# Convolution sums of an even mixer in PSUM, two taps per GpSimd add, and another order of its output projection

## The chip, the cores and the metric

The kernel runs on one core of a Trainium2 chip. The metric is the device time of one execution in microseconds (us); several runs are taken and their median is given. The engines are named as in the profile: PE is TensorE (matmuls; PEld its weight loads), DVE is VectorE, ACT is ScalarE, POOL is GpSimd, and SP issues most of the transfers.

## The reference

Two blocks on a sequence of 256 tokens of width 1024, in float32. The first block has two layers, each with a feed-forward part, a mixer and a second feed-forward part; the mixer of layer 0 is the even mixer, that of layer 1 a gated linear attention. The second block has one layer with two kinds of attention and a feed-forward part. The change touches the even mixer alone:

```python
def even_mixer(h, w_in, w_out, dw_w, dw_b, ln_g, ln_b):
    proj = h @ w_in
    q, k, v, u, gate = jnp.split(proj, [SB_WIDTH, 2 * SB_WIDTH, 3 * SB_WIDTH, 3 * SB_WIDTH + CONV_CH], axis=-1)
    a_out = merge_heads(stick_breaking_attention(
        split_heads(q, SB_HEADS), split_heads(k, SB_HEADS), split_heads(v, SB_HEADS)))
    c = u * jax.nn.sigmoid(gate)
    c = causal_depthwise_conv(c, dw_w, dw_b)          # 31 taps, 512 channels
    c = jax.nn.silu(layer_norm(c, ln_g, ln_b))
    return jnp.concatenate([a_out.astype(h.dtype), c], axis=-1) @ w_out
```

There are 8 heads of 64 columns. The attention and the convolution are independent of each other until the output projection, which takes the heads as the first 512 of its input rows and the convolution as the other 512.

## The kernel before

**Products.** Every float32 product of the large projections is made of three matmuls: each operand is split into a rounded part and the rest (hi and lo of a weight, xh and xl or mh and ml of an activation), and hi·high, lo·high and hi·low are summed in PSUM (lines 269, 270, 271).

**Weights.** They arrive in chunks of 512 KB. For a chunk SP issues the transfer into one of four buffers `raw` (line 226), ACT writes `hi` (line 246), DVE writes `lo` = raw − hi (line 247), and the buffer takes the transfer of the chunk four places on as soon as its `lo` is done. `nxt` hands chunks to the matmuls and, each time, converts ahead up to a distance that `DEPTH` gives; while `side` holds `conv_some`, each chunk that is handed over also issues some taps of the convolution.

**The order** in which each engine gets its instructions is the order of the program (`manual_schedule`); an engine waits at an instruction until its operands are there, with all that stands behind it.

**The even mixer** runs from about 204 to 325 us of the span. A projection by `wp` is 48 matmuls. First come the convolution's inputs (`hu`, `hg`, twice, for the channel groups 0, 1 and 2, 3 of 128 channels each); behind the first pair stands `rows`, which turns the row scales of the input's norm into a tile `rb` by two small matmuls (line 432) of diagonal tiles `dg` from ACT (line 431). The gated product goes into `cpad` (line 829). Then `qk(0)` and `qk(1)` project queries and keys (`qT` line 844, `kT` line 847), and the attention runs over four pairs of heads: `z_` (logits, on PE from qT and kT, line 856), `e_` (ACT: abs, exp, ln; DVE: max and add, line 873), `c_` (sums of logarithms on PE, exp on ACT), `o_` (the values on PE, `mh` by ACT line 897, `ml` by DVE line 898).

The 31 taps of each channel group are laid between these steps by the numbers in TD, TP, TC and TE. Groups 0 and 2 run on DVE alone: even taps sum into `y`, odd ones into `yb` (line 793, both in SBUF), and the last step adds the two (line 795). Groups 1 and 3 run on two engines: ACT multiplies one tap (line 803) and POOL adds it to `y` (line 804).

**The end of the mixer.** `part` issues the first piece of the output projection (chunk rows of `mh` 0 and 1, all four of its PSUM banks: 24 matmuls, in the order hi·mh, lo·mh, hi·ml for each). Then the last taps, `c_(2)`, `c_(3)`, `conv_mean` (PE sums over channels, line 905; DVE subtracts, line 907; ACT squares), `o_(2)`, `o_(3)`, `conv_var` (layer norm, silu on ACT, and the split into mh and ml, lines 532 and 533), a second `part`, and the rest in `pieces`. PSUM has 8 banks, handed out in turn by `pb()`.

Of the kernel before, what the change touches and what calls it, by code (L numbers as in the profile page):

```python
# [12 lines left out]
AF = mybir.ActivationFunctionType  # L13
ALU = mybir.AluOpType
AX = mybir.AxisListType.X

S = 256
# [5 lines left out]
CW = 31  # L23
# [4 lines left out]
NH = 3  # L28
TB = (5, 6)
KO = (0, 4, 1, 5, 2, 6, 3, 7)  # L30
TD, TP, TC = (3, 2), 3, ((5, 6), (5, 6), (4, 6), (4, 5))
PRE = (1, 1, 2)
PRT = ((0, 0, 0), (1, 0, 0))
PRF = (0, 0, 2)
CT, CS = (2, 2), (0, 1)
CU = (0, 1, 2)
DEPTH = (14, (10, 9), (10, 10), (10, 10))
NT = 2
LO, CL = ((1, 0), (1, 1)), 1
PG = 5  # L40
# [3 lines left out]
NW = 8  # L44
KS = (1, 3, 5, 7)
TE = (2, 0, 4, 4)
W2 = dict(qa=0, ka=512, va=1024, iq=1536, ik=2048, iw=2112, qr=2120, kr=2632,
          vr=3144, gr=4168, ga=5192, gb=6216)

# [51 lines left out]
def weight_plan(a):  # L101
    plan = []

    def cols(name, w, c0, n, k0=0, nk=8):
        plan.append((name, w[k0 * 128:(k0 + nk) * 128, c0:c0 + n].rearrange("(k p) c -> p k c", p=128), nk, n))

    def tall(name, w, c0):
        for k0 in (0, 4):
            cols(name, w, c0, 256, k0, 4)

    def wide(name, w, c0=0, n=1024, nk=8):
        for cc in range(c0, c0 + n, 512):
            for k0 in range(0, nk, 2):
                cols(name, w, cc, 512, k0, 2)
# [41 lines left out]
    w = a["w_in_2"]  # L156
    wide("va", w, W2["va"], 512)
    wide("rv", w, W2["vr"], 512)
    cols("ik", w, W2["ik"], 72)
    for c in range(2):  # L160
        tall("iq", w, W2["iq"] + 256 * c)
    for c in range(2):
        tall("rq", w, W2["qr"] + 256 * c)
        tall("rk", w, W2["kr"] + 256 * c)
    wide("rv", w, W2["vr"] + 512, 512)
# [23 lines left out]
def block_kernel(ctx: ExitStack, tc: tile.TileContext, a: dict, out: bass.AP, upto: int = 99):  # L189
    nc = tc.nc  # L190
    pe, act, dve, pool = nc.tensor, nc.scalar, nc.vector, nc.gpsimd
# [8 lines left out]
    def pb():  # L200
        return ps.tile([128, 512], F32, tag="pb", name="pb")

    def pp():
        return [pb(), pb()]
# [4 lines left out]
    def s4(shape, dt=F32, name="s4"):  # L209
        return wk.tile(shape, dt, tag="s4", name=name, bufs=NS4)  # L210

    def s2(shape, dt=F32, name="s2"):
        return wk.tile(shape, dt, tag="s2", name=name, bufs=NS2)
# [3 lines left out]
    raw_t, cv_t = {}, {}  # L217
    pos = {"dma": 0, "cv": 0, "use": 0, "depth": DEPTH[0]}
    side = []
# [31 lines left out]
    def nxt(*names, ahead=True):  # L251

        i = pos["use"]
        for d_, nm in enumerate(names):
            assert plan[i + d_][0] == nm, (plan[i + d_][0], nm)
        n = i + len(names)
        feed_cv(max(n, min(i - 1 + pos["depth"], pos["cv"] + len(names) + 1)) if ahead else n)
        pos["use"] += len(names)
        for _ in names:
            for f in list(side):  # L260
                f()
        r = [cv_t.pop(i + d_) for d_ in range(len(names))]
        return r if len(r) > 1 else r[0]
# [4 lines left out]
    def mm3(o, lh, ll, rh, rl, start, stop):  # L268
        pe.matmul(o, lh, rh, start=start, stop=False)  # L269
        pe.matmul(o, lh, rl, start=False, stop=False)  # L270
        pe.matmul(o, ll, rh, start=False, stop=stop)  # L271

    def tsl(t):
        return slice(t * 128, (t + 1) * 128)
# [276 lines left out]
    def two(z):  # L551
        return z.rearrange("p (c s) -> p c s", c=2)
# [4 lines left out]
    def smm(o, t, ch, k0, nk, xh, xl):  # L557
        for k in range(ch[0].shape[1]):
            kk = k0 + k
            mm3(o, xh[:, kk, tsl(t)], xl[:, kk, tsl(t)], ch[0][:, k], ch[1][:, k], kk == 0, kk == nk - 1)  # L560
# [21 lines left out]

    def sproj_tail(name, xh, xl):

        f = [pp(), pp()]
        pos["depth"] = DEPTH[0]
        todo = {t: {n: [0, 1, 2, 3] for n in range(2)} for t in range(2)}
        chs = {}

        def one(t, n, i):  # L590
            smm(f[t][n], t, chs[i][n], 2 * i, 8, xh, xl)

        def part(leave=()):

            i = len(chs)
            chs[i] = nxt(name, name)
            for t in range(2):
                for n in range(2):
                    if (t, n) not in leave:
                        todo[t][n].remove(i)  # L600
                        one(t, n, i)

        def pieces():
            i0 = len(chs)
            cs = nxt(*[name] * (2 * (4 - i0)), ahead=False)
            for i in range(i0, 4):
                chs[i] = cs[2 * (i - i0):2 * (i - i0) + 2]
            return lambda t: [(lambda n=n, i=i: one(t, n, i)) for n in range(2) for i in todo[t][n]]
        return f, part, pieces
# [3 lines left out]
    part = const.tile([128, 192], F32, name="part")  # L613
# [143 lines left out]
    def even_mixer(nz):  # L757
# [17 lines left out]
        for c in range(4):  # L775
            pool.memset(cpad[c][:, :CW - 1], 0.0)
        y = s4([128, 4, S], name="y")
        yb2 = s2([128, 2, S], name="yb")
        yb = [yb2[:, c] for c in range(2)]
        dq, aq, pts = [], [], []  # L780

        def tap(c, k, on_dve):
            src = cpad[c][:, k:k + S]
            w = cols_[:, 1, 4 * k + c:4 * k + c + 1]
            b = cols_[:, 2, 24 + c:25 + c]
            if on_dve:
                o = yb[c // 2] if k % 2 else y[:, c]
                if k == 0:
                    dve.tensor_scalar(o, src, w, b, op0=ALU.mult, op1=ALU.add)
                elif k == 1:  # L790
                    dve.tensor_scalar(o, src, w, None, op0=ALU.mult)
                else:
                    dve.scalar_tensor_tensor(o, in0=src, scalar=w, in1=o, op0=ALU.mult, op1=ALU.add)
                if k == CW - 1:
                    dve.tensor_tensor(o, o, yb[c // 2], op=ALU.add)
            elif k == 0:
                act.activation(y[:, c], src, AF.Identity, scale=w, bias=b)
            else:
                if not pts:
                    p2 = s2([128, 2, S], name="pt")  # L800
                    pts.extend([p2[:, 0], p2[:, 1]])
                pt = pts.pop(0)
                act.activation(pt, src, AF.Copy, scale=w)
                pool.tensor_tensor(y[:, c], y[:, c], pt, op=ALU.add)

        calls = []

        def conv_some(n=None, m=TP):
            if n is None:
                n = TD[len(calls) % len(TD)]  # L810
                calls.append(n)
            for q, n_ in ((dq, n), (aq, m)):
                for _ in range(min(n_, len(q))):
                    tap(*q.pop(0))

        for c in range(2):
# [15 lines left out]
            if c == 0:  # L832
                side.append(conv_some)
        pos["depth"] = DEPTH[1][1]
        act.preload_act_table_set("natural_log_exp_and_others")
# [28 lines left out]
        def e_(hp):  # L864
            pz = st[hp]
            e = s4([128, 2, 384], name="ze")
            for i in range(2):
                act.activation(e[:, i], pz[i][:, :384], AF.Abs)
            act.activation(e, e, AF.Exp, scale=-1.0)
            act.activation(e, e, AF.Ln, bias=1.0)  # L870
            conv_some(TE[hp], 0)
            for i in range(2):
                dve.scalar_tensor_tensor(e[:, i], in0=pz[i][:, :384], scalar=0.0, in1=e[:, i],
                                         op0=ALU.max, op1=ALU.add)
            st[hp] = pz, e
# [68 lines left out]
        z_(3)  # L944
        o_(1)
        f, part, pieces = sproj_tail("ho", mh, ml)
        e_(2)
        conv_some(*TC[3])
        e_(3)
        part()  # L950
        conv_some(99, 99)
        y2 = s4([128, 4, S], name="y2")
        c_(2)
        c_(3)
# [1 line left out]
        o_(2)  # L956
        o_(3)
        conv_var()
        part(LO)
        return f, pieces()  # L960


    def odd_mixer(nz):
        x = nz.x
        pos["depth"] = DEPTH[2][1]
        sc_ = s4([128, 2, 4, 128], name="scores")
# [197 lines left out]
        for t in range(2):  # L1164
# [3 lines left out]
            gated(t, 1)  # L1168
            rows_T(t, oy[t], oh, ol, [0])
        f, part, pieces = sproj_tail("go", oh, ol)  # L1170
        part()
        for t in range(2):
# [5 lines left out]
    def second(nz):  # L1178
# [315 lines left out]
        for t in range(2):  # L1494
            rows_T(t, ga[t], xh3, xl3)
        f, _, pieces = sproj_tail("wo", xh3, xl3)
        return f, pieces()

# [31 lines left out]
    for k in range(8):  # L1530
        nz.evac1(0, k)
        for i in (k // 4 * 2, k // 4 * 2 + 1):
            hi, lo = (z[:, k % 4] for z in cv_t[i])
# [7 lines left out]
    for i in range(6):  # L1541
        l, s = divmod(i, 3)
        gb = brow(a["norm_g"][l, 2 * s + 1])
        if s == 1:
            pos["depth"] = DEPTH[1 + l][0]
            f, pieces = (odd_mixer if l else even_mixer)(nz)
        else:
            f, pieces = ffn(nz, each)
# [11 lines left out]
        if upto == i:  # L1560
            dump()
            return
    pos["depth"] = DEPTH[3][0]
    f, pieces = second(nz)
# [9 lines left out]
    f, pieces = ffn(nz)  # L1574
    for t in range(2):
# [5 lines left out]
        y = [s2([128, 512], name="tm") for _ in range(2)]  # L1581
# [33 lines left out]
```

## Time and profile before

| | |
|---|---|
| median of 3 runs | 1476.81 us (1474.69 to 1477.07) |
| the profiled execution | 1476.34 us |
| its span, and its mean granted clock of PE | 1474.6 us, 0.992 |
| PE busy | 1440.0 us, 98% |
| PEld busy | 1314.8 us, 89% |
| DVE busy | 1000.3 us, 68% |
| ACT busy | 764.5 us, 52% |
| POOL busy | 259.5 us, 18% |

The span is the time between the first and the last instruction of the profiled execution; 1.7 us of its own time lie around it. Busy shares are means over all stages, and the even mixer is some 8% of the span.

### The profile page before, as it was taken

The page shows a single profiled execution, that of the slowest core. Times are in us where ns is not written, and L with a number is a line of the kernel's source. Part 1 is how long each engine was busy: PE and PEld are TensorE (multiplying, and loading weights), DVE is VectorE, ACT ScalarE, POOL GpSimd, SP SyncE. Part 2 cuts the span into 40 slices and gives each one's busy share as a digit, 9 for nine tenths or more (in the row PEclk, how much of TensorE's full clock was granted, in tenths as well). Part 3 has the DMA queues.
Part 4 walks back from the last instruction along what each step waited for, and adds up shares of the span by engine and source line. Part 5 has one row for each costly group of instructions (what it writes and reads, how often), then busy time and mean ns, then how long its engine had stood idle before and what let it go on. Part 6 is the DMA issues. An engine that isn't in the chain of part 4 may idle for free. (4 is left out here: it accounts for less than half of the span.)

```text
span 1474.6 us, 24444 instructions
## 1 busy us (share of the span) xinstructions
PE 1440.0 (98%) x9623; PEld 1314.8 (89%) x9623; DVE 1000.3 (68%) x1348; ACT 764.5 (52%) x1182; POOL 259.5 (18%) x339
## 2 busy tenths in 40 slices
PE   9999998699999999999999999999999999999997
PEld 8999988579999999999888899998988877899997
DVE  6777658977776667766577677765596865566542
ACT  6554356756543364443663655545643664565431
POOL 3010025812000031000234110001132230200001
PEclk9999999899999999999999999999999999999999
DMA  8887644227887568775542488763565554387540
GB/s 276 275 279 250 188 144 130 71 86 241 286 260 234 172 223 265 231 237 173 163 144 72 129 282 261 259 207 116 164 198 169 165 170 157 101 262 240 183 129 29
DMA packets 194948, 281.03 MB, mean 191 GB/s; under 512 B 12381, under 2 KB 148241, under 8 KB 194834
## 3 DMA queue, kind: packets, MB, share of 16 engines
q1 hardware_dynamic: 184386, 248.87, 53.5%
q0 software_dynamic: 10048, 30.03, 6.2%
q8 instruction: 75, 1.23, 0.3%
q10 hardware_dynamic: 400, 0.57, 0.1%
q14 instruction: 39, 0.32, 0.1%
HBM read 277.90 MB, written 1.05 MB: 189 GB/s over the span
## 5 line engine op out<-in xcount | busy, mean ns | idle before, releaser
L247 DVE TENSOR_TENSOR lo<-raw,hi 128x1024 fp32r<-128x1024 f32 (+1 forms) x461 | 549.5, 1219 | 237.2 <-ACT hi L246 204.0
L246 ACT ACTIVATE hi<-raw 128x1024 fp32r<-128x1024 f32 (+1 forms) x472 | 477.4, 1037 | 206.4 <-PE pb L271 69.2
L269 PE MATMUL pb<-xh,hi 128*128 128x256 f32 x1968 | 558.4, 284 | 0.1
L271 PE MATMUL pb<-xh,lo 128*128 128x256 f32 x1968 | 556.8, 283 | 0.0
L270 PE MATMUL pb<-xl,hi 128*128 128x256 f32 x1968 | 556.8, 283 | 0.0
L269 PEld LDWEIGHTS pb<-xh,hi 128*128 128x128 f32 x1968 | 376.3, 191 | 3.4 <-issue 1.3
L270 PEld LDWEIGHTS pb<-xl,hi 128*128 128x128 f32 x1968 | 376.4, 191 | 2.0
L271 PEld LDWEIGHTS pb<-xh,lo 128*128 128x128 f32 x1968 | 376.3, 191 | 0.2
L269 PE MATMUL pb<-hi,hh 128*128 128x512 f32 x440 | 172.1, 391 | 0.0
L270 PE MATMUL pb<-lo,hh 128*128 128x512 f32 x440 | 171.7, 390 | 0.0
L271 PE MATMUL pb<-hi,hl 128*128 128x512 f32 x440 | 171.2, 389 | 0.0
L626 POOL DMA_DIRECT2D ada<-in_w_ada_dram x96 | 51.8, 542 | 452.0 <-PE pb L271 278.8
L532 ACT ACTIVATE hh<-u 128x512 fp32r<-128x512 f32 x50 | 31.6, 632 | 134.4 <-DVE u L745 132.5
L271 PEld LDWEIGHTS pb<-hi,hl 128*128 128x128 f32 x440 | 82.6, 188 | 17.5
L269 PEld LDWEIGHTS pb<-hi,hh 128*128 128x128 f32 x440 | 82.8, 188 | 15.9
L270 PEld LDWEIGHTS pb<-lo,hh 128*128 128x128 f32 x440 | 82.8, 188 | 15.3
L269 PE MATMUL pb<-hi,xh 128*128 128x512 f32 x224 | 91.5, 408 | 0.0
L271 PE MATMUL pb<-hi,xl 128*128 128x512 f32 x224 | 88.1, 393 | 0.0
L270 PE MATMUL pb<-lo,xh 128*128 128x512 f32 x224 | 88.0, 393 | 0.0
L730 ACT ACTIVATE sg<-sg 128x512 f32<-128x512 f32 x40 | 25.3, 632 | 109.8 <-DVE sg L729 109.8
L631 DVE SCALAR_TENSOR_TENSOR adacc<-ada,sc,adacc 128x512 f32<-128x512 f32 x84 | 63.0, 750 | 2.0
L331 POOL TENSOR_TENSOR rs_y<-rs_v,mhalf 128x1 f32<-128x1 f32 x30 | 16.9, 564 | 259.0 <-DVE rs_v L330 258.0
(314 smaller groups left out, 1726.2 us busy)
## 6 DMA issues: line engine op xcount, KB each, us to landing
raw<-in_ffn_w_in_dram SPq DMA_DIRECT2D x176, 512.0 KB, 5.0
raw<-in_ffn_w_out_dram SPq DMA_DIRECT2D x88, 512.0 KB, 4.7
raw<-in_w_in_dram SPq DMA_DIRECT2D x56, 512.0 KB, 4.2
ada<-in_w_ada_dram POOLq DMA_DIRECT2D x96, 256.0 KB, 4.5
raw<-in_gla_w_in_dram SPq DMA_DIRECT2D x24, 512.0 KB, 4.2
raw<-in_w_ffn_gate_dram SPq DMA_DIRECT2D x22, 512.0 KB, 4.8
raw<-in_w_ffn_up_dram SPq DMA_DIRECT2D x22, 512.0 KB, 5.0
raw<-in_w_ffn_down_dram SPq DMA_DIRECT2D x22, 512.0 KB, 4.0
```

The lines of the kernel that those rows point to most:

```text
L246: act.activation(hv, r, AF.Copy)
L247: lo_on.tensor_tensor(lv, r, hv, op=ALU.subtract)
L269: pe.matmul(o, lh, rh, start=start, stop=False)
L270: pe.matmul(o, lh, rl, start=False, stop=False)
L271: pe.matmul(o, ll, rh, start=False, stop=stop)
L331: pool.tensor_tensor(y, v, mhalf[:, :1], op=ALU.pow)
L532: act.activation(hi, full, AF.Copy)
L626: pool.dma_start(t, w_ada[kt * 128:(kt + 1) * 128, cb * 512:(cb + 1) * 512])
L631: dve.scalar_tensor_tensor(ada["acc"], in0=t, scalar=sc[:, kt:kt + 1], in1=ada["acc"], op0=ALU.mult, op1=ALU.add)
L730: act.activation(sg, sg, AF.Silu)
```

## The change

Six things:

1. A DVE group's two sums stand in one PSUM bank (its two halves of 256 columns) instead of in SBUF. The last tap and the closing add write `y` in SBUF.
2. An ACT group's taps go in pairs: ACT writes two products side by side (`pt`, 512 columns), and one POOL add of 512 columns puts them on a pair of sums `ya`; two adds of 256 columns close the group.
3. The first `part` uses three of the four banks of the output projection and issues all its matmuls with `mh` ahead of those with `ml`: 12, and then 6. The second `part` leaves out the same bank (18 matmuls instead of 12), and the banks are taken from the pool one by one as they are first used.
4. The last taps are issued ahead of that `part`, so ahead of the conversions in it.
5. TC lays the taps between the steps a little differently.
6. `DEPTH` of the first two projections rises from 10 to 12.

```diff
-TD, TP, TC = (3, 2), 3, ((5, 6), (5, 6), (4, 6), (4, 5))
+TD, TP, TC = (3, 2), 3, ((5, 6), (4, 6), (3, 6), (4, 6))
...
-DEPTH = (14, (10, 9), (10, 10), (10, 10))
+DEPTH = (14, (12, 9), (10, 10), (10, 10))
...
+HL = ((1, 1),)
...
-        f = [pp(), pp()]
+        f = [[None, None], [None, None]]
...
+        def bank(t, n):
+            f[t][n] = f[t][n] or pb()
+            return f[t][n]
+
         def one(t, n, i):
-            smm(f[t][n], t, chs[i][n], 2 * i, 8, xh, xl)
-
-        def part(leave=()):
+            smm(bank(t, n), t, chs[i][n], 2 * i, 8, xh, xl)
+
+        def part(leave=(), low_last=False):
 
             i = len(chs)
             chs[i] = nxt(name, name)
...
+            tn = [(t, n) for t in range(2) for n in range(2) if (t, n) not in leave]
+            for t, n in tn:
+                todo[t][n].remove(i)
+                if not low_last:
+                    one(t, n, i)
+            for low in range(2 if low_last else 0):
+                for t, n in tn:
+                    o = bank(t, n)
+                    for k in range(2):
+                        kk = 2 * i + k
+                        hi, lo = (z[:, k] for z in chs[i][n])
+                        if low:
+                            pe.matmul(o, xl[:, kk, tsl(t)], hi, start=False, stop=kk == 7)
+                        else:
+                            pe.matmul(o, xh[:, kk, tsl(t)], hi, start=kk == 0, stop=False)
+                            pe.matmul(o, xh[:, kk, tsl(t)], lo, start=False, stop=False)
...
         def tap(c, k, on_dve):
...
             if on_dve:
-                o = yb[c // 2] if k % 2 else y[:, c]
+                if k == 0:
+                    acc[c] = two(pb())
+                o = acc[c][:, k % 2]
...
+                elif k < CW - 1:
+                    dve.scalar_tensor_tensor(o, in0=src, scalar=w, in1=o, op0=ALU.mult, op1=ALU.add)
                 else:
-                    dve.scalar_tensor_tensor(o, in0=src, scalar=w, in1=o, op0=ALU.mult, op1=ALU.add)
-                if k == CW - 1:
-                    dve.tensor_tensor(o, o, yb[c // 2], op=ALU.add)
+                    dve.scalar_tensor_tensor(y[:, c], in0=src, scalar=w, in1=o, op0=ALU.mult, op1=ALU.add)
+                    dve.tensor_tensor(y[:, c], y[:, c], acc.pop(c)[:, 1 - k % 2], op=ALU.add)
             elif k == 0:
-                act.activation(y[:, c], src, AF.Identity, scale=w, bias=b)
+                acc[c] = [s2([128, 2, S], name="ya"), None]
+                act.activation(acc[c][0][:, 0], src, AF.Identity, scale=w, bias=b)
+            elif k == 1:
+                act.activation(acc[c][0][:, 1], src, AF.Copy, scale=w)
+            elif k < CW - 1:
+                ya = acc[c][0]
+                if k % 2 == 0:
+                    acc[c][1] = s2([128, 2, S], name="pt")
+                pt = acc[c][1]
+                act.activation(pt[:, k % 2], src, AF.Copy, scale=w)
+                if k % 2:
+                    pool.tensor_tensor(ya, ya, pt, op=ALU.add)
             else:
...
-                pool.tensor_tensor(y[:, c], y[:, c], pt, op=ALU.add)
+                pool.tensor_tensor(pt, ya[:, 1], pt, op=ALU.add)
+                pool.tensor_tensor(y[:, c], ya[:, 0], pt, op=ALU.add)
...
-        part()
         conv_some(99, 99)
+        part(HL, True)
...
-        part(LO)
+        part(HL)
```

Three places show how the order of instructions moves. On ACT, ahead of the diagonal tiles of `rows` (the second projection of the mixer is being multiplied on PE then), before:

```order
L773 ACTIVATE cr<-zmf 128x384
L246 ACTIVATE hi<-raw 128x1024 x3
L431 ACTIVATE dg<-ident,rs_y 128x128 x2
L827 ACT_TABLE_LOAD
L827 ACTIVATE sgg<-sgg 128x512
L246 ACTIVATE hi<-raw 128x1024 x2
```

and in the changed kernel, whose line numbers are one to some thirty higher:

```order
L789 ACTIVATE cr<-zmf 128x384
L247 ACTIVATE hi<-raw 128x1024 x5
L432 ACTIVATE dg<-ident,rs_y 128x128 x2
L853 ACT_TABLE_LOAD
L853 ACTIVATE sgg<-sgg 128x512
L247 ACTIVATE hi<-raw 128x1024 x2
```

Two more conversions stand ahead of `dg`. On DVE, up to the first `kT`, before:

```order
L793 SCALAR_TENSOR_TENSOR y<-cpad,cols,y 128x256
L844 SCALAR_TENSOR_TENSOR qT<-pb,rb 128x512
L247 TENSOR_TENSOR lo<-raw,hi 128x1024 x2
L793 SCALAR_TENSOR_TENSOR yb<-cpad,cols,yb 128x256
L793 SCALAR_TENSOR_TENSOR y<-cpad,cols,y 128x256
L793 SCALAR_TENSOR_TENSOR yb<-cpad,cols,yb 128x256
L793 SCALAR_TENSOR_TENSOR y<-cpad,cols,y 128x256
L793 SCALAR_TENSOR_TENSOR yb<-cpad,cols,yb 128x256
L847 TENSOR_TENSOR kT<-pb,rb 128x512
L247 TENSOR_TENSOR lo<-raw,hi 128x1024 x2
```

and in the changed kernel:

```order
L809 SCALAR_TENSOR_TENSOR pb<-cpad,cols,pb 128x256 x5
L870 SCALAR_TENSOR_TENSOR qT<-pb,rb 128x512
L248 TENSOR_TENSOR lo<-raw,hi 128x1024
L809 SCALAR_TENSOR_TENSOR pb<-cpad,cols,pb 128x256 x5
L873 TENSOR_TENSOR kT<-pb,rb 128x512
L248 TENSOR_TENSOR lo<-raw,hi 128x1024 x2
```

The number of taps between is the same and one conversion is gone from between (`pb` is the PSUM bank). On DVE at the end of the mixer, before:

```order
L873 SCALAR_TENSOR_TENSOR ze<-pb,ze 128x384 x2
L247 TENSOR_TENSOR lo<-raw,hi 128x1024 x3
L793 SCALAR_TENSOR_TENSOR yb<-cpad,cols,yb 128x256
L793 SCALAR_TENSOR_TENSOR y<-cpad,cols,y 128x256
L793 SCALAR_TENSOR_TENSOR yb<-cpad,cols,yb 128x256
L793 SCALAR_TENSOR_TENSOR y<-cpad,cols,y 128x256
L795 TENSOR_TENSOR y<-y,yb 128x256
L907 TENSOR_TENSOR y<-y,pb 128x256 x4
```

and in the changed kernel:

```order
L899 SCALAR_TENSOR_TENSOR ze<-pb,ze 128x384 x2
L809 SCALAR_TENSOR_TENSOR pb<-cpad,cols,pb 128x256 x5
L811 SCALAR_TENSOR_TENSOR y<-cpad,cols,pb 128x256
L812 TENSOR_TENSOR y<-y,pb 128x256
L248 TENSOR_TENSOR lo<-raw,hi 128x1024 x3
L933 TENSOR_TENSOR y<-y,pb 128x256 x4
```

The three conversions now stand behind the last tap and ahead of the subtraction of the mean, instead of ahead of the last four taps.

## Rows read from the trace of the kernel before

**Rows 1.** Waits of PE over the whole span: total us, times, longest

```profile
PE pb L856 <- DVE kT L847: 9.0, 2, 7.3
PE pb L271 <- DVE ml L898: 6.4, 2, 3.8
PE pb L1081 <- DVE last L1057: 2.1, 1, 2.1
PE pb L269 <- ACT mh L532: 1.2, 1, 1.2
```

**Rows 2.** Windows: PE, PEld, DVE, ACT, POOL busy (x); PEclk, DMA share, GB/s

```profile
254.00:306.60 52.60, 36.43 (x218) 28.75 (x218) 52.57 (x70) 36.02 (x71) 38.29 (x43) 0.87 0.24 73
...
261.20:265.20 4.00, 3.96 (x18) 2.86 (x18) 4.00 (x4) 2.21 (x4) 3.80 (x3) 0.50 0.35 115
...
291.70:295.70 4.00, 4.00 (x10) 3.13 (x11) 4.00 (x7) 3.93 (x6) 3.61 (x6) 0.50 0.00 0
```

**Rows 3.** Timelines of DVE and PE up to the second kT: start, length

```profile
236.75 2.89 DVE L247 TENSOR_TENSOR lo<-raw,hi 128x1024 fp32r<-128x1024 f32 x2
...
247.22 1.23 DVE L247 TENSOR_TENSOR lo<-raw,hi 128x1024 fp32r<-128x1024 f32 x1 [1.61 <-ACT hi L246]
...
256.18 0.94 DVE L793 SCALAR_TENSOR_TENSOR yb<-cpad,cols,yb 128x256 f32<-128x256 f32 x1
...
260.51 0.68 DVE L847 TENSOR_TENSOR kT<-pb,rb 128x512 f32<-128x512 f32 x1
...
261.24 1.65 PE L856 MATMUL pb<-qT,kT 64*128 64x256 f32 x8 [7.29 <-DVE kT L847]
...
279.76 0.92 PE L856 MATMUL pb<-qT,kT 64*128 64x256 f32 x8 [1.74 <-DVE kT L847]
```

**Rows 4.** Timelines of POOL and DVE at the mixer's end

```profile
270.51 28.31 POOL L804 TENSOR_TENSOR y<-y,pt 128x256 f32<-128x256 f32 x31 [3.31 <-ACT pt L803]
...
287.73 0.41 DVE L898 TENSOR_TENSOR ml<-pb,mh 128x256 fp32r<-128x256 f32 x1
...
301.54 3.48 DVE L247 TENSOR_TENSOR lo<-raw,hi 128x1024 fp32r<-128x1024 f32 x3
...
305.74 0.47 DVE L793 SCALAR_TENSOR_TENSOR yb<-cpad,cols,yb 128x256 f32<-128x256 f32 x1
306.13 0.47 DVE L793 SCALAR_TENSOR_TENSOR y<-cpad,cols,y 128x256 f32<-128x256 f32 x1
306.64 0.42 DVE L795 TENSOR_TENSOR y<-y,yb 128x256 f32<-128x256 f32 x1
308.29 1.41 DVE L907 TENSOR_TENSOR y<-y,pb 128x256 f32<-128x256 f32 x4 [1.22 <-PE pb L905]
```

**Rows 5.** Groups of POOL's adds by shape: busy, mean ns of one

```profile
L804 POOL TENSOR_TENSOR y<-y,pt 128x256 f32<-128x256 f32 x60 | 54.7, 912 | 31.3 <-ACT pt L803 26.8
...
L1342 POOL TENSOR_TENSOR sgr<-sgr,brow 128x512 f32<-128x512 f32 x4 | 5.2, 1291 | 25.1 <-ACT sgr L1341 25.0
...
L1069 POOL TENSOR_TENSOR ex<-cs 128x512 f32<-128x512 f32 x6 | 10.5, 1751 | 0.0
```

**Rows 6.** Timelines of ACT, PE and DVE around the diagonal tiles

```profile
218.90 2.94 ACT L246 ACTIVATE hi<-raw 128x1024 fp32r<-128x1024 f32 x3
...
224.20 0.60 PE L432 MATMUL pb<-dg,ones 128*128 128x128 f32 x4
...
228.63 0.76 DVE L829 TENSOR_TENSOR cpad<-sgg,us 128x256 f32<-128x256 f32 x2 [2.04 <-ACT sgg L827]
```

**Rows 7.** Transfers of line 226 from 195 to 262: issues, time to landing

```profile
221.23 2.64 SPq L226 DMA_DIRECT2D raw<-in_hyb_w_in_dram  x3
...
DMA to landing us min/median/max: 3.5/4.6/5.6
```

**Rows 8.** Windows behind PE's wait at line 1081 (columns as in rows 2)

```profile
766.00:768.00 2.00, 1.85 (x10) 1.73 (x11) 2.00 (x4) 0.58 (x1) 0.00 (x0) 0.76 0.40 156
768.00:770.00 2.00, 2.00 (x6) 1.57 (x5) 2.00 (x4) 0.04 (x2) 0.00 (x0) 0.50 0.21 14
```

More of the change, by code (lines that the diff above doesn't have):

```diff
@@ L588, in sproj_tail @@
         chs = {}
+        def bank(t, n):
+            f[t][n] = f[t][n] or pb()
+            return f[t][n]
         def one(t, n, i):
-            smm(f[t][n], t, chs[i][n], 2 * i, 8, xh, xl)
-        def part(leave=()):
+            smm(bank(t, n), t, chs[i][n], 2 * i, 8, xh, xl)
+        def part(leave=(), low_last=False):
             i = len(chs)
             chs[i] = nxt(name, name)
[L597 to L601, printed above, removed]
+            tn = [(t, n) for t in range(2) for n in range(2) if (t, n) not in leave]
[14 more added lines that the diff above has]
+                            pe.matmul(o, xh[:, kk, tsl(t)], lo, start=False, stop=False)
         def pieces():
@@ L777, in even_mixer @@
         y = s4([128, 4, S], name="y")
-        yb2 = s2([128, 2, S], name="yb")
-        yb = [yb2[:, c] for c in range(2)]
-        dq, aq, pts = [], [], []
+        dq, aq, acc = [], [], {}
         def tap(c, k, on_dve):
@@ L791, in tap @@
                     dve.tensor_scalar(o, src, w, None, op0=ALU.mult)
-                else:
-                    dve.scalar_tensor_tensor(o, in0=src, scalar=w, in1=o, op0=ALU.mult, op1=ALU.add)
-                if k == CW - 1:
-                    dve.tensor_tensor(o, o, yb[c // 2], op=ALU.add)
+                elif k < CW - 1:
+                    dve.scalar_tensor_tensor(o, in0=src, scalar=w, in1=o, op0=ALU.mult, op1=ALU.add)
+                else:
+                    dve.scalar_tensor_tensor(y[:, c], in0=src, scalar=w, in1=o, op0=ALU.mult, op1=ALU.add)
+                    dve.tensor_tensor(y[:, c], y[:, c], acc.pop(c)[:, 1 - k % 2], op=ALU.add)
             elif k == 0:
-                act.activation(y[:, c], src, AF.Identity, scale=w, bias=b)
-            else:
[L799 to L802, printed above, removed]
+                acc[c] = [s2([128, 2, S], name="ya"), None]
[10 more added lines that the diff above has]
+                    pool.tensor_tensor(ya, ya, pt, op=ALU.add)
+            else:
+                ya, pt = acc.pop(c)[0], s2([128, S], name="pt")
                 act.activation(pt, src, AF.Copy, scale=w)
-                pool.tensor_tensor(y[:, c], y[:, c], pt, op=ALU.add)
+                pool.tensor_tensor(pt, ya[:, 1], pt, op=ALU.add)
+                pool.tensor_tensor(y[:, c], ya[:, 0], pt, op=ALU.add)
         calls = []
```

## The prediction

> **What bounds the kernel now.** The page comes first: PE is busy 98% of the span, so only PE's idle time and the time it runs at a low clock can be won. The list of PE's waits then says where they are [rows 1]: the four waits for `kT` and `ml` (15.4 us), and one of 1.2 us for `mh`, all lie in the even mixer. Who is late there is seen in the windows [rows 2]: from 254 to 306.6 us DVE is busy 52.57 of 52.60 us, PE 36.4, and the granted clock is 0.87. [...]
>
> Why DVE is late is read from its single instructions. A tap takes 0.94 us while POOL adds [rows 3] and 0.47 when POOL has stopped, with one starting every 0.39 [rows 4]. POOL adds nearly without a gap (31 in 28.31 us). A tap alternates between `y` and `yb`, so it never follows the tap whose sum it needs; where one does follow its own producer (the closing add behind the last tap) the start is 0.51 behind [rows 4]. A DVE instruction with one operand in PSUM takes the same beside POOL as an SBUF add without it: `ml` 0.41 at 287.73, against 0.42 for the closing add [rows 4].
>
> **The change, part by part.**
>
> *Taps in PSUM.* What is not in the trace is a DVE instruction that writes PSUM. Both halves of a bank belong to one tile, and in the built program each tap waits for the tap right ahead of it. I take 0.51 a tap, the start-to-start of the dependent pair, with no slowing by POOL, since only `cpad` is left in SBUF, and the row with one PSUM operand shows none. Lower bound 0.39 (dependence hidden); upper bound 0.88, today's start-to-start beside POOL (0.94 less the overlap of 0.06), should POOL still get in the way. The value lies near the low end because the `ml` row does.
>
> [...]
>
> *The rows step (DEPTH).* Ahead of `dg` ACT now converts five chunks instead of three. The three took 2.94 us [rows 6], 0.98 each. The fifth chunk waits for its transfer: the first of the three issues at 221.23 [rows 7], when a buffer is free. Landing takes 3.5 to 5.6 us there, median 4.6; I take 4.2, a little under it, because fewer transfers are under way at that place than later in the stretch. Landed 225.4, converted 226.4, `dg` +0.44: PE's matmul of line 432, which ran at 224.20 without a wait [rows 6], now starts at 226.85. **PE waits 2.65 us** (2.0 to 4.1 over the range of landings). Behind it in PE's queue stand the second `hu` and all of the rest; `rb`, and with it all DVE work of the mixer, is late by the same. This part removes nothing from the path there; of the two conversions, one is gone from between `cpad` and `kT`.
>
> *First kT.* `cpad` starts at 228.63 and ends at 229.4 [rows 6]; now 232.05. To `kT`, DVE has 20 taps x 0.51 = 10.2, five conversions 1.23 to 1.45 each (the alone and the beside-POOL value [rows 3]) 6.5, four evacuations x 0.65 (`kT`'s 0.68 less overlap) 2.6, the second `cpad` 0.76, waits for ACT 1.6 (the wait at 247.22 [rows 3]): 21.7, end 253.75. PE comes to line 856 at 261.24 − 7.29 + 2.65 = 256.60. The wait of 7.29 is gone with 2.9 us to spare; if the taps stayed at 0.88, 20 x 0.37 = 7.4 us later, 4.5 of it would be back.
>
> *Second kT.* From 256.60, PE needs 279.76 − 261.24 − 1.74 = 16.78 us in the old trace, less the 2 us of the slow clock: 271.4. DVE between the two `kT` (4 conversions at 1.4, 11 taps and the first of the next group at 0.51, closing add, four `ze` at 0.5, `qT`, `kT`: about 16 with its waits) ends at about 270.7. Cover 0.7, so this wait goes too, but barely.
>
> *The DVE tail sets the end.* From 270.7: 30 taps x 0.51 = 15.3, two `ml` 0.75, four `ze` 1.9, a wait of 0.5 for the last pair's logarithm on ACT, closing add 0.42: **289.6**. The first `part` no longer stands in front of it: its 18 matmuls run from about 276 to 281.3 (1.5 us of wait for the second `mh` among them), and the six with `ml` come last, so the waits of 3.8 and 2.5 for `ml` go. POOL does 14 adds of 512 columns a group instead of 30 of 256. Alone such an add takes 1.29, contended 1.75 [rows 5]; I take 1.3, since what no longer slows DVE's taps should not slow POOL either, and POOL then ends at about 288.3, ahead of the tail. At 1.75, 14 x 0.45 = 6.3 later, it would end at 294.6 and cost some 2.5 us.
>
> *Conversions behind the last taps.* Three conversions in 3.48 us [rows 4] from 289.6: 293.05. In that time PE runs `conv_mean` (line 905), which cost DVE 1.22 us of waiting before line 907 in the old order [rows 4]. Line 907 therefore starts at 293.05 instead of 308.29: **−15.2 us**. [...]
>
> *From there on* nothing changes: six matmuls moved from the first `part` behind `conv_var` at 0.23 us (1.4 us) fill the wait of 1.2 for `mh` [rows 1], and what follows is paced by ACT's silu as before. Nothing.
>
> *Clock.* A lone wait of 2.07 us at line 1081 [rows 1] was followed by granted clocks of 0.76 and 0.50 in the next two stretches of 2 us [rows 8], 1.5 us lost; the one of 1.74 at 278 was not. The new wait of 2.65 may do the same: 0 to 1.8, half of it, **+0.9**.
>
> **Sum.** 1476.34 (profiled) − 15.2 + 0.9 = 1462.0; the median of the runs is 0.5 above the profiled execution, so 1462.5. What a measurement here can tell from no change is 0.2%, 3 us.
>
> **The rivals.**
>
> *A. No new wait at the rows step, or cheaper taps.* If the fifth chunk lands early, 2.65 + 0.9 come back: 1459. Taps at 0.39 alone give little, since ACT's last logarithm and its three `hi` then hold line 907 within 1 us: 1461.5. Both: 1458. For it: the shortest landing is 3.5. Against: the issue hangs on a free buffer.
>
> *B. Dearer taps, or slow POOL adds.* At 0.60 a tap the 30 of the tail cost 2.7 more: 1465. At 0.70, 5.7 in the tail and little before it: 1468. POOL at 1.75: 1465. For it: no row writes PSUM, and the 912 ns of POOL's adds is a contended value itself [rows 5].
>
> *C, the other side: POOL still delays the taps.* If a tap that reads `cpad` from SBUF is still held up by each POOL add, the add that holds it up is twice as wide: today's delay is 0.88 − 0.39 = 0.49 us, so 0.98 for 512 columns, and a tap that meets one takes 1.37. POOL is busy most of the mixer, and about one tap in two meets an add (28 adds, 62 taps): 28 x 0.98 = 27 us on DVE against 62 x 0.49 = 30 before, and every tap is 0.12 dearer by its dependence (7 us). With the new wait of 2.65 the sum is about +10: 1486. It decides when the mean tap is above about 0.85. Against: the `ml` row beside POOL.
>
> *D. It does nothing in the time:* a mean tap near 0.82 with the rows step paid gives 1474 to 1479. Nothing in the trace points at that value.
>
> [...]
>
> **How the numbers follow.** The forecast's own case (1460 to 1464): 0.60. A 0.15, B 0.15, D 0.04, C 0.06. Faster by over 0.2%: 0.60 + 0.15 + 0.15 = 0.90; the same 0.04; slower 0.06. The range leaves out C, D and the far end of B: from 1457 (A with a little of the slack behind it) to 1470 (B beyond 0.70).
>
> **What would show it.** Taps of line 809 at 0.5 apart also where POOL runs, POOL's adds of 512 columns at 1.3, no wait of PE for `kT`, a wait of PE of 2.0 to 4.1 at line 433 (the old 432) with the fifth `hi` and its transfer ahead of it, and line 933 (the old 907) at about 293, 15 us earlier, straight behind the three conversions. Wrong would be: taps above 0.6, above all those that meet a POOL add; a wait at `kT` that stays; POOL as the last before `conv_mean`; or time lost again behind line 933.

## The result, and the profile after

The changed kernel takes 1458.67 us in the median of 4 runs (1458.45 to 1460.42), the kernel before 1476.78 on the same occasion: a ratio of 0.988, with an interval of 0.9863 to 0.9896. That is 18.1 us less; 14.3 were forecast. The time lies inside the range of 1457 to 1470, but below the forecast's own case of 1460 to 1464. The profiled execution took 1458.62 us, its span 1456.9.

The waits of PE over the whole span of the changed kernel (total us, times, longest):

```profile
PE pb L1107 <- DVE last L1083: 2.1, 1, 2.1
PE pb L433 <- ACT dg L432: 2.0, 2, 1.6
...
PE pb L616 <- ACT mh L923: 1.0, 1, 1.0
PE pb L878 <- DVE ze L899: 1.0, 1, 1.0
...
PE pb L939 <- ACT y L934: 0.7, 1, 0.7
...
PE pb L931 <- DVE y L812: 0.2, 1, 0.2
```

No `kT` and no `ml` is left in it, where there were 15.4 us [rows 1]. New are the rows step (line 433, the old 432) and waits of about 1 us each for `mh` and `ze`. The same window as in [rows 2]:

```profile
254.00:306.60 52.60, 49.62 (x307) 39.28 (x306) 47.08 (x85) 45.29 (x93) 29.32 (x23) 1.00 0.26 80
```

PE is now busy 49.6 of 52.6 us instead of 36.4, at full clock throughout. DVE's groups from 270 to 287 us, and POOL's, in the changed kernel (busy us, mean ns | idle):

```profile
L825 POOL TENSOR_TENSOR ya<-ya,pt 128x512 f32<-128x512 f32 x12 | 15.4, 1280 | 0.9
...
L809 DVE SCALAR_TENSOR_TENSOR pb<-cpad,cols,pb 128x256 f32<-128x256 f32 x27 | 13.2, 489 | 0.8
```

and its DVE timeline at the two `kT` and at the end, with POOL's adds there, beside [rows 3, 4]:

```profile
253.08 0.68 DVE L873 TENSOR_TENSOR kT<-pb,rb 128x512 f32<-128x512 f32 x1
...
269.48 0.68 DVE L873 TENSOR_TENSOR kT<-pb,rb 128x512 f32<-128x512 f32 x1
...
280.03 4.16 DVE L809 SCALAR_TENSOR_TENSOR pb<-cpad,cols,pb 128x256 f32<-128x256 f32 x8
284.10 1.01 DVE L899 SCALAR_TENSOR_TENSOR ze<-pb,ze 128x384 f32<-128x384 f32 x2
285.03 2.58 DVE L809 SCALAR_TENSOR_TENSOR pb<-cpad,cols,pb 128x256 f32<-128x256 f32 x5
287.64 0.48 DVE L811 SCALAR_TENSOR_TENSOR y<-cpad,cols,pb 128x256 f32<-128x256 f32 x1
288.16 0.42 DVE L812 TENSOR_TENSOR y<-y,pb 128x256 f32<-128x256 f32 x1
288.50 3.49 DVE L248 TENSOR_TENSOR lo<-raw,hi 128x1024 fp32r<-128x1024 f32 x3
291.90 1.41 DVE L933 TENSOR_TENSOR y<-y,pb 128x256 f32<-128x256 f32 x4
```

```profile
267.24 18.95 POOL L825 TENSOR_TENSOR ya<-ya,pt 128x512 f32<-128x512 f32 x14
```

Eight taps beside a POOL that never stops take 4.16 us, 0.52 each. The closing add, the three conversions and line 933 follow without a gap. Line 933 starts at 291.90 instead of 308.29.

**A ruler for the mixer.** The executions of one kernel scatter by two to four us here, and more in some, so single executions are also compared over the mixer alone: from ACT's copy of the identity at its start to ACT's first square of its output. Its rows in the timelines of ACT of three profiles: the kernel before, the changed one, and the changed one run again.

```profile
213.81 0.31 ACT L772 ACTIVATE cr<-ident 128x128 fp32r<-128x128 f32 x1
...
321.19 0.57 ACT L342 ACTIVATE sq<-pb 128x512 f32<-128x512 f32 x1
```

```profile
214.10 0.31 ACT L788 ACTIVATE cr<-ident 128x128 fp32r<-128x128 f32 x1
...
304.33 0.57 ACT L343 ACTIVATE sq<-pb 128x512 f32<-128x512 f32 x1
```

```profile
213.14 0.31 ACT L788 ACTIVATE cr<-ident 128x128 fp32r<-128x128 f32 x1
...
303.36 0.58 ACT L343 ACTIVATE sq<-pb 128x512 f32<-128x512 f32 x1
```

That is 107.38 us before and 90.23 and 90.22 after: 17.15 less, and the same to a hundredth in two executions of the changed program. The table holds this length for every kernel that was run; the words in it are those of the experiments below. The medians are of four occasions, on which the kernel before had 1476.5 to 1476.8.

| kernel | median us | mixer us | against before |
|---|---|---|---|
| before | 1476.78 | 107.38 | |
| changed | 1458.67 | 90.23 | −17.15 |
| changed, sums in SBUF | 1475.28 | 107.70 | +0.32 |
| before, sums in PSUM only | 1470.66 | 102.79 | −4.59 |
| before, sums in PSUM and three banks | 1463.65 | 94.15 | −13.23 |
| before, pairs on POOL only | 1480.17 | 112.11 | +4.73 |
| changed, four banks | 1469.94 | 100.78 | −6.60 |
| changed, one tap per POOL add | 1462.80 | 91.56 | −15.82 |
| changed, part ahead of the last taps | 1462.66 | 93.20 | −14.18 |
| changed, DEPTH 10 | 1462.15 | 93.55 | −13.83 |
| changed, two banks for the sums | 1475.13 | 105.33 | −2.05 |
| changed, early rows step | 1458.85 | 88.15 | −19.23 |
| changed, early rows step, two conversions later | 1459.01 | 87.58 | −19.80 |

### The profile page after: what moved, and what is told of

The parts are those of the page before. It is cut to its first block, busy times and chain, and to the rows that moved or that the text cites. A ratio compares the mean times of both kernels' runs of the same rounds, so it can differ in the third digit from the quotient of the medians.

```text
span 1456.9 us, 24390 instructions
## 1 busy us (share of the span) xinstructions
PE 1434.3 (98%) x9623; PEld 1311.0 (90%) x9623; DVE 983.5 (68%) x1348; ACT 763.6 (52%) x1182; POOL 247.1 (17%) x311
## 4 chain that ended last, share of the span: by engine, by line
PE 89%; DVE 4%; ACT 3%; DMA 2%; issue 2%; POOL 0%; SPq 0%; POOLq 0%; DVEq 0%
PE pb L270 27%; PE pb L272 27%; PE pb L271 27%; DVE lo L248 2%; PE pb L701 1%; PE pb L700 1%; PE pb L704 1%; ACT hi L247 1%; PE pb L393 1%; DMA raw<-in_ffn_w_out_dram 1%; ACT pt L823 0%; DVE pb L809 0%; DMA raw<-in_ffn_w_in_dram 0%; DVE ex L1083 0%; DMA raw<-in_w_in_dram 0%
## 5 line engine op out<-in xcount | busy, mean ns | idle before, releaser
L271 PEld LDWEIGHTS pb<-lo,hh 128*128 128x128 f32 x440 | 82.8, 188 | 15.4
L761 DVE TENSOR_TENSOR u<-sg,pb 128x512 f32<-128x512 f32 x50 | 34.1, 682 | 40.2 <-PE pb L272 39.5
```

Of the source, the lines that this page charges most:

```text
L761: dve.tensor_tensor(u, sg, two(pb_), op=ALU.mult)
```

## The experiments

Theory 1, the prediction's: sums in PSUM free DVE's taps from POOL's adds, and DVE was the bound. Theory 2: the new order makes the gain. Theory 3: the halved number of POOL adds makes it.

### Sums back in SBUF, and pairs alone

```diff
-                    acc[c] = two(pb())
+                    acc[c] = wk.tile([128, 2, S], F32, tag="ac", name="ac", bufs=1)
```

(A tile of its own; one buffer fewer, NS2 = 15, makes room.)

> The changed kernel with the two sums of a DVE group back in SBUF, one tile of its own; all else stays (pairs on POOL, order, DEPTH). Theory 1 (the sums in PSUM make the gain: taps no longer slowed by POOL's adds, DVE was the bound): the taps beside POOL go back to about 0.9 us, the wait of PE for kT comes back with 4 to 7 us, the time is 1470 to 1480. Theory 2 (the new order of the output projection and of the last taps makes the gain): 1460 to 1463, though taps are slow. Theory 3 (fewer POOL adds make the gain): the taps are slowed in part only, 1462 to 1467.

Measured 1475.28, a ratio of 0.9987 [0.9977, 0.9998] to before: everything but PSUM brings next to nothing. PE waits 4.9 us for `kT` and 6.8 for `ml` again, and a tap takes 0.86 us in the mean:

```profile
PE pb L616 <- DVE ml L924: 5.0, 1, 5.0
PE pb L882 <- DVE kT L873: 4.9, 1, 4.9
...
PE pb L614 <- DVE ml L924: 1.8, 1, 1.8
```

Theories 2 and 3 fall.

The other half of it: the kernel before with only POOL's adds in pairs (the lines of the diff's ACT branch, `yb` in its own tile, one buffer fewer here too).

> The kernel before with POOL's adds in pairs of taps and nothing else. Theory 1: taps with both tensors in SBUF are slowed by wide adds as by narrow ones, the wait for kT stays at 5 to 8 us: 1474 to 1479. Theory 3 (fewer adds make the gain): 1462 to 1467.

Measured 1480.17, ratio 1.003 [1.0018, 1.0042]: slower than before, beyond what theory 1 said. Its waits for `kT` and `ml`, its groups from 281 to 294 us, and its DVE timeline there:

```profile
PE pb L865 <- DVE kT L856: 10.6, 1, 10.6
PE pb L271 <- DVE ml L907: 10.2, 2, 9.3
```

```profile
L808 POOL TENSOR_TENSOR ya<-ya,pt 128x512 f32<-128x512 f32 x11 | 14.5, 1323 | 0.9
L793 DVE SCALAR_TENSOR_TENSOR y<-cpad,cols,y 128x256 f32<-128x256 f32 x5 | 7.5, 1503 | 0.0
L793 DVE SCALAR_TENSOR_TENSOR yb<-cpad,cols,yb 128x256 f32<-128x256 f32 x4 | 5.9, 1485 | 0.0
```

```profile
289.78 1.48 DVE L793 SCALAR_TENSOR_TENSOR y<-cpad,cols,y 128x256 f32<-128x256 f32 x1
291.19 1.48 DVE L793 SCALAR_TENSOR_TENSOR yb<-cpad,cols,yb 128x256 f32<-128x256 f32 x1
292.60 1.49 DVE L793 SCALAR_TENSOR_TENSOR y<-cpad,cols,y 128x256 f32<-128x256 f32 x1
294.01 0.41 DVE L907 TENSOR_TENSOR ml<-pb,mh 128x256 fp32r<-128x256 f32 x1
...
295.43 0.47 DVE L793 SCALAR_TENSOR_TENSOR y<-cpad,cols,y 128x256 f32<-128x256 f32 x1
```

One tap starts every 1.41 us, as often as POOL starts an add (12 in 16.97 us from 278.25 on). Where POOL adds without a gap here, a tap with both tensors in SBUF gets through once per add, and wider adds make it slower: 1.48 us beside adds of 512 columns, 0.94 beside adds of 256 [rows 3]. `ml`, right between them and with an operand in PSUM, takes 0.41. This is the mechanism of the prediction's rival C; it holds for taps in SBUF, and not for taps into PSUM (0.52 from tap to tap beside POOL in the changed kernel). A tap alone takes 0.47, so of a POOL add's 1.32 us about 1.0 is lost to the tap, not all of it.

### Sums in PSUM, and the banks for them

The kernel before with the DVE branch of the diff, and nothing else:

> The kernel before with the two sums of a DVE group in a PSUM bank and nothing else of the change. Theory 1: taps at 0.51, no wait of PE for kT, no wait of 2.65 or 1.6 at the rows step; the waits for ml behind the old first part shrink, and about 11 to 15 us are gained: 1462 to 1466. Theory 2: the waits for ml stay at 6 us and the tail moves little, 1470 to 1477. Theory 3: POOL's 30 adds a group bound the tail as before: 1470 to 1477.

Measured 1470.66, ratio 0.996 [0.9946, 0.9973]. The time is the one that theories 2 and 3 gave, not the 1462 to 1466 of theory 1. The waits say why: `kT` cost PE only 0.8 us, as theory 1 said, but a wait came that no theory had: for a bank.

```profile
PE pb L269 <- DVE y L796: 11.6, 1, 11.6
PE pb L271 <- DVE ml L899: 2.2, 2, 1.3
...
PE pb L857 <- DVE kT L848: 0.8, 2, 0.4
```

The releaser is the closing add (line 796 there), and the one that waits is the first product into the fourth bank of the output projection: `z_(2)` and `z_(3)` hold four banks, the running sums one, the projection three, and that makes eight. The same from the other side, the changed kernel with four banks:

```diff
-        part(HL, True)
+        part((), True)
...
-        part(HL)
+        part(LO)
```

> The changed kernel with all four banks of the output projection in the first part, as before, and the old LO in the second; high-first order and last taps in front stay. Theory (the sums in PSUM take one of 8 banks until the closing add, so that the fourth bank must wait for it): PE waits at the fourth bank from about 279 until the closing add at 288 to 290, 8 to 10 us, c_(2) and c_(3) stand behind it, line 933 comes 5 to 8 us later: 1464 to 1468. Rival (the bank count does nothing, the kernel before with sums in PSUM waited for something else): 1458 to 1459.

Measured 1469.94, a little above what was said, with the wait again at that place:

```profile
PE pb L616 <- DVE y L812: 9.4, 1, 9.4
```

And the kernel before with sums in PSUM and one bank left out in both parts (`part(((1, 1),))` twice, banks taken as they are used):

> The kernel before with the sums of a DVE group in PSUM and three banks in both parts of the output projection; no pairs on POOL, old order of the first part and of the last taps, old TC and DEPTH. If sums in PSUM and the bank that they need are the core of the change, PE's wait of 11.6 us for the fourth bank is gone and most of the gain is here: 1462 to 1465. If the pieces add up as they did when each was undone alone (DEPTH 3.5, place of the last taps 3, pairs 0.6 of the 16), it is 1467 to 1469. Rival: another wait takes the bank's place, 1470 as without the third-bank change.

Measured 1463.65, ratio 0.9922 [0.9903, 0.9941], the mixer 13.2 us shorter: about three quarters of the whole in two edits that belong together. The wait for the fourth bank is gone; of the earlier waits of PE `ml` (2.2), the closing add (2.8) and `kT` (0.8) are left. (The profiled execution itself took 1468.64, 5 us above the median: its mixer began 4.5 us later, which the ruler leaves out.)

### The pace of 0.52

```diff
-                    acc[c] = two(pb())
-                o = acc[c][:, k % 2]
+                    acc[c] = [pb()[:, :S], pb()[:, :S]]
+                o = acc[c][k % 2]
```

> The changed kernel with the two sums of a DVE group in two PSUM banks instead of the two halves of one. If the 0.51 us from tap to tap is the wait for the tap right ahead in the same bank, the pace falls to 0.40, DVE's tail is 3 us shorter, and ACT then holds line 933 to a gain of about 1: 1457.5. If 0.51 is what a tap into PSUM costs, the pace stays and the time too, 1458.7. If the second bank is missed by z_ or by the output projection, PE waits for a bank: 1459 to 1463.

The first and the third case came true at once, the third far beyond the 1459 to 1463 that was said. Five taps and twice eight in this kernel's DVE timeline, POOL's adds, and PE's waits:

```profile
243.95 2.05 DVE L809 SCALAR_TENSOR_TENSOR pb<-cpad,cols,pb 128x256 f32<-128x256 f32 x5
...
271.87 3.22 DVE L809 SCALAR_TENSOR_TENSOR pb<-cpad,cols,pb 128x256 f32<-128x256 f32 x8
...
286.46 3.22 DVE L809 SCALAR_TENSOR_TENSOR pb<-cpad,cols,pb 128x256 f32<-128x256 f32 x8
```

```profile
275.06 17.49 POOL L825 TENSOR_TENSOR ya<-ya,pt 128x512 f32<-128x512 f32 x13 [7.10 <-ACT pt L823]
```

```profile
PE pb L616 <- DVE y L811: 9.1, 1, 9.1
PE pb L270 <- DVE qT L870: 5.6, 1, 5.6
```

(3.22 − 0.47) / 7 = 0.39 from tap to tap, at 271.87 with POOL idle and at 286.46 with POOL adding: a tap into PSUM is as fast as one into SBUF alone, and POOL's adds do not reach it. The 0.52 is the wait for the tap right ahead in the same bank. In the program of the changed kernel each tap waits for the one right ahead; with two banks, and likewise with the two sums as halves of one SBUF tile (the first experiment), it waits for the one before that. The seven taps of that first experiment behind POOL's last add show the pace without PSUM:

```profile
297.27 2.84 DVE L809 SCALAR_TENSOR_TENSOR ac<-cpad,cols,ac 128x256 f32<-128x256 f32 x7
```

That is 0.39 to 0.40 again, so it is the shared bank, not a shared tile, that makes a tap wait. But the second bank is missing elsewhere, PE waits 14.7 us, and the median is 1475.13 (ratio 0.9995 [0.9985, 1.0004]). The 0.12 us a tap cost less than the second bank does.

### What each smaller edit is worth

DEPTH back at 10 (its 12 holds from the mixer's start up to the projection of the queries, so for five projections and not for the first two alone):

> The changed kernel with DEPTH of the second projection back at 10. By my prediction's step the wait of PE at line 433 (1.6 us in the changed kernel) goes, and since everything of the mixer hangs on it, the time is 1457.0. Rival: two conversions come back between the first cpad and the first kT (2.6 us of DVE), the first kT comes about 1 us too late for PE, and the wait moves there: 1458 to 1459. A second rival: the wait at line 433 has another cause than the fifth conversion and stays.

Measured 1462.15, the mixer 3.3 us longer: the prediction's step is refuted, and the rival too small. The wait at line 433 is gone, but PE waits for both `kT`:

```profile
PE pb L882 <- DVE kT L873: 2.9, 2, 2.3
```

Two conversions return between the first `cpad` and the first `kT`, and behind a wait of 2.3 the mean granted clock of the window from 254 to 306.6 is 0.97 instead of 1.00.

The first part ahead of the last taps, its products in the old order (still three banks):

> The changed kernel with the first part (still three banks) ahead of the last taps and with each product's three matmuls together, so the three conversions stand ahead of the last six taps, as before. My prediction gave the conversions' place 1.2 us (the wait for the mean's matmuls in front of line 933): 1460. Rival (this order is what makes the gain): 1464 or more. Rival the other way (it costs nothing, PE's other waits hide it): 1458.7.

Measured 1462.66; the mixer 3.0 us longer, where 1.2 was said. Line 931 (the old 905) now waits for the closing add, which the conversions delay:

```profile
PE pb L931 <- DVE y L812: 2.8, 1, 2.8
```

One tap per POOL add, the old ACT branch:

> The changed kernel with POOL's adds of 256 columns, one tap each, as before; DVE's sums stay in PSUM. By my prediction taps no longer meet POOL's adds, so an add takes 0.8 instead of 0.91 us, a group's 30 take 24 instead of 20.4 us, POOL is the last before the mean's matmuls by about 3 us: 1460 to 1462. Theory 3 (fewer adds are what makes the gain): 1467 or more. If POOL has slack after all: 1458.7.

Measured 1462.80 in the median, the mixer 1.3 us longer. DVE's taps are untouched (488 ns in the mean), and POOL is the last before the mean's matmuls (line 922 there):

```profile
PE pb L922 <- POOL y L821: 2.3, 1, 2.3
```

This profile, 1461.13, is 2.5 us above that of the changed kernel: 1.3 in the mixer, and up to 1.7 behind PE's wait at 749 to 751 us, where the granted clock was 0.69 from 750 to 754 us and 0.88 from 754 to 758 (0.31 and 0.12 of 4 us each; more on that place below). So what the pairs are shown to be worth is the 1.3; why the median lies another 1.7 above the profile stays open.

The three do not add up. Undone one at a time they cost 3.3, 3.0 and 1.3 us of the mixer, 7.6 together; but all of them and the new TC bring only 3.9 on top of the sums in PSUM and the three banks (17.15 against 13.23). The 1467 to 1469 that was worked out for that kernel by adding them up did not come. The new TC was not run by itself.

### Candidates

The diagonal tiles ahead of the conversions, and the rows step and `us` ahead of the second projection:

```diff
+        nz.diag()
         cf, cr = s2([128, 3, 128], name="cf"), s2([128, 512], F32R, name="cr")
...
             if c == 0:
-                p = wp("hg", x)
                 nz.rows()
             us = s2([128, 2, S], name="us")
             dve.tensor_tensor(us, two(pu), bc2(x.rb), op=ALU.mult)
-            if c:
-                p = wp("hg", x)
+            p = wp("hg", x)
```

(`diag` writes the two tiles that `rows` wrote.)

> The changed kernel with the diagonal tiles of the rows step issued on ACT ahead of the five conversions, its matmuls in front of the second projection, and the first product of the convolution in front of two conversions on DVE. The wait of 1.6 us at line 433 goes. If all of the mixer hangs on DVE from there, the gain is what the first sigmoid's input gains, 1.06 us (it then waits for the fifth lo): 1457.6. If PE's other waits grow by as much: 1458.7. If the whole 1.6 is won: 1457.0.

And that with two of the three `lo` held back until behind the last two `ml`:

```diff
+        pos["hold"] = pos["cv"]
         part(HL, True)
+        pos["hold"] = 0
...
         o_(3)
+        while held:
+            held.pop(0)()
         conv_var()
```

> The changed kernel with the early rows step, and two of the three lo conversions in front of line 933 put behind the last two ml, so that the mean is subtracted about 2 us earlier on DVE. PE is busy with the mean's and the last heads' matmuls by then, so only its wait for the squares (0.69 us) can be won besides the 1.6 of the early rows step: 1456.4 by the trace at the end of the mixer, 2.3 us ahead of the changed kernel. Rival: the held conversions make DVE late for the layer norm, and it is 1457 to 1458.

The wait at the mixer's rows step is gone in both, and the mixer is 2.1 and 2.65 us shorter than in the changed kernel. The medians, 1458.85 and 1459.01, do not show it: the changed kernel has 1458.67, and 1459.31 when it ran beside the second candidate, so that neither is shown to be better. Part of it is seen to go elsewhere. The first candidate's waits hold

```profile
PE pb L440 <- ACT dg L432: 1.4, 2, 0.9
```

which is the rows step of two later feed-forward parts, where the changed kernel waits 0.4 in all. Ahead of the first of them the conversion on ACT waits 2.92 us for its transfer. Where the rest of the 2 us goes was not followed.

### The changed kernel again

> The changed kernel again, beside the last candidate on one chip, and for the clock behind PE's wait of 2.06 us at line 1107 (the old 1081). If the low clock of 1.7 us there is a matter of the single execution, this profile may show it though the first one of the changed kernel did not, with PE's marks ahead of it equal to within 0.2 us: 1458.7, or 1460.4 where it is lost.

Measured 1459.31 (1457.3 to 1461.38), ratio 0.9888 [0.9871, 0.9905]. Its clock behind the lone wait of 2.05 us at line 1107, in windows, and that of the first profile of the same program:

```profile
748.00:752.00 4.00, 3.64 (x13) 3.35 (x14) 4.00 (x7) 0.60 (x1) 0.00 (x0) 0.57 0.29 110
752.00:756.00 4.00, 4.00 (x28) 3.58 (x27) 1.34 (x2) 2.80 (x4) 0.23 (x1) 1.00 0.73 257
```

```profile
750.00:754.00 4.00, 3.91 (x22) 3.45 (x23) 4.00 (x6) 1.29 (x2) 0.00 (x0) 1.00 0.25 84
```

One execution ran at 0.57 behind that wait, the other at 1.00: 0.43 of 4 us, or 1.7 us of full clock, lost by the execution and not by the program. The profile with the loss is no longer than the other (1458.55 against 1458.62), because it came to line 1107 1.7 us earlier; that the marks ahead would be equal, and the time 1460.4, was not borne out.

The profile before had the loss too [rows 8]: PE takes 5.34 us there from line 1081 to the next line 1099, and 3.71 us from line 1107 to line 1125 in the first profile after. Its line 1081 starts at 766.15, and line 1107 in the first profile after at 750.09. So of the 17.7 us between these two spans 16.1 were won ahead of that line, and 1.6 at the clock there are not the change's doing.

## Why the prediction was right, point by point

The mechanism was right: DVE's taps were held by POOL's adds, and in PSUM they are not. The size was too small by 3.8 us, and the measured time is the 1459 of rival A, whose condition, no new wait at the rows step, did not hold: 1.6 us of it came.

**Taps in PSUM: right.** 0.52 from tap to tap beside POOL (0.51 taken), by the dependence, as argued. With the dependence taken away a tap into PSUM starts every 0.39 us (two banks for the sums), as one into SBUF did [rows 4].

**POOL's adds: right.** 1.28 us in the mean in the tail (1.3 taken), with POOL done just ahead of the closing add. That the 1.75 of line 1069 is an add slowed by contention, as the upper bound took it, is not shown by any row; its six took 1.04 to 2.12 us.

**First and second kT: right.** The first is done at 253.76 (253.75 worked out), the second at 270.16 (270.7), and neither is waited for. That the first agrees to a hundredth is luck: `cpad` ended 0.4 sooner, and from there to `kT` DVE took 22.1 us instead of 21.7. The 2 us of slow clock taken off PE's way to the second are half of the 4.00 us that PE was busy at 0.50 [rows 2]: eight matmuls of line 856 took 1.65 us there and 0.92 at 279.76 [rows 3], where the clock was 1.00. In the changed kernel it is 1.00 from 254 to 306.6 us.

**The rows step: sized too high, and read wrongly as a whole.** PE waited 1.60 us, not 2.65, and less than the 2.0 at which the text began its range. The fifth conversion started 3.6 us behind the issue at 221.26, close to the shortest landing of [rows 7] (3.5), and not 4.2; that is 0.6 of the difference. PE also came to the line 0.5 later than in the trace before.

```profile
224.88 1.06 ACT L247 ACTIVATE hi<-raw 128x1024 fp32r<-128x1024 f32 x1 [2.07 <-DMA raw<-in_hyb_w_in_dram]
225.85 0.68 ACT L432 ACTIVATE dg<-ident,rs_y 128x128 f32<-128x128 f32 x2
```

The text counted this edit as a cost alone ("removes nothing from the path", one conversion gone from between `cpad` and `kT`). Two are gone, seven before and five after, the sum used the five without crediting them, and with DEPTH at 10 the mixer is 3.3 us longer. So the edit was a gain.

**The tail: right in its make-up.** Line 933 comes at 291.90, 16.4 us earlier; 15.2 were forecast. The difference is the second `kT`, done 0.5 sooner, and the last logarithm, for which DVE waited nothing instead of 0.5. The smaller wait at the rows step hardly reaches this chain: the first `cpad` was 0.4 sooner, and the first `kT` was not.

**Conversions behind the last taps: undersized.** 1.2 us taken; with the rest of the first part's order undone too, 3.0.

**From there on: nearly.** The first square of the mixer's output follows line 933 by 12.43 us, where it followed the old line 907 by 12.90 [rows 4]: PE has the last heads' matmuls behind it when the squares come (it waits 0.7 for them), and before it had not.

**Clock: wrong.** No granted clock below 1.00 followed the new wait (1.00 in each 2 us from 224 to 234), so the +0.9 did not come, and the lone loss at 766 us, taken as given, was absent from the first profile.

**The sum.** The forecast for the profiled execution was 1462.0, and it took 1458.6. Of these 3.4 us the tail makes 1.15, the stretch behind it 0.5, the two clock terms 0.9 and 1.6; 0.8 were lost again between the mixer and line 1107, 0.4 of them at the rows step of a feed-forward part. The other 0.4 of the 3.8 is the distance from profile to median, 0.5 in the forecast and 0.05 here. So 1.6 of it is the chance of one execution.

## What to carry to other kernels

When VectorE and GpSimd both run two-tensor SBUF instructions all the time, as in this mixer, look at the pace of VectorE's: if it equals the pace of GpSimd's (1.41 us for both here with the pairs alone), move one operand of VectorE's to PSUM (0.52 us from tap to tap here), and widen GpSimd's instructions only after that. Widening first made this kernel slower (1480.17 us, a ratio of 1.003), and widening after it made it faster (1.3 us of the mixer). Count the PSUM banks before taking one: the sums alone gave about a quarter of the gain (4.59 of 17.15 us of the mixer), and half of it (8.64) came when the output projection gave up a bank.

An edit that adds a wait has to be charged together with the work that it takes from elsewhere on the path.

## What was not expected of the hardware

A tap in SBUF next to POOL adds of 512 columns takes 1.48 us, with a pace of 1.41, against 0.47 alone and 0.94 next to adds of 256. A wait of PE of just over 2 us at one place was followed by a granted clock of 0.57 over 4 us in one execution and of 1.00 in another of the same program, which is worth 1.7 us of full clock here; how much of the scatter of the executions it makes was not tried.
